# A two-layer decoder trunk: attention of both token tiles of a head at once on all 128 rows, weight roundings pinned in the mixer, tiles moved to multiples of 512 bytes

## The chip, the cores and the metric

The kernel runs on one NeuronCore of a Trainium2 chip. The metric is device time in microseconds (us) of one execution; lower is better. A profile is one execution taken by the hardware profiler: its span goes from the first to the last instruction, and the execution's own time is a little longer than the span. Engines are named as the profile names them: PE is TensorE's matmul, PEld its weight load, DVE is VectorE, ACT is ScalarE, POOL is GpSimd, SP is SyncE, which issues most DMAs.

## What is computed

256 tokens of width 2048 go through two layers. Cut to what matters here, a layer is:

```python
h = rmsnorm(x, attn_norm_g)
q, k, v, gate_b, gate_c, conv_in = split(h @ w_in)          # each 1024 wide
q, k = rmsnorm(q per 64), rmsnorm(k per 64)                 # 8 heads x 2 maps x 64
s = q . k / 8 + bias(relative distance), masked to the past
p = softmax(s)[map 0] - lam * softmax(s)[map 1]             # per head
attn = rmsnorm(p @ v per head) * (1 - lam_init)
conv = gate_b * causal_conv3(gate_c * conv_in)
x = x + concat([attn, conv]) @ w_out
x = x + relu(rmsnorm(x) @ w_up)**2 @ w_down                 # 8192 wide inside
```

All inputs and outputs are float32. The big products are made in float32r, a rounded float32 that PE multiplies in one pass: each operand is split into a rounded part (hi) and what the rounding leaves (lo), and a product is hi*hi + hi*lo + lo*hi.

## The kernel before, in words

**Stages.** For each of the two layers `mixer` (L599) makes everything up to `w_out`, and `mlp` (L667) the rest. In `mixer`, for each half of the heads (four of eight), `linear` (L325) makes q, then k, then v, each 16 row blocks of 128 by 2 token tiles by 3 terms. Then come four column groups of `gate_c` and `conv_in` and four of `gate_b`, by `linear_t` (L344), which turns the product round: the weights are the stationary operand, and the moving one is 512 columns wide (hi and lo of the activations) against hi and 256 against lo. Then `w_out` by `linear`. The multiplication in `mlp` uses `up_part` (L799), which has `linear_t`'s form, `product` (L846) and L969.

**Weights.** `Weights.halves` (L274) takes a loaded block of 128 rows by 1024 numbers and rounds it: an ACT copy to `whi` (L282), then a DVE subtraction to `wlo` (L283). `take` (L310) makes a block's halves three blocks ahead of its use. A block feeds 12 matmuls in `linear`, 8 wide and 8 narrow ones in `linear_t`.

**The order of the work.** PE's order is written out by hand. Small work is a generator that `Background.tick` (L74) carries on a piece at a time: `linear` ticks once in 6 matmuls, `linear_t` four times in a block of 16. `yield n` means: go on n ticks later. The other engines' instructions are ordered by a planner with a cost model of its own; `late(ins)` (L118) pins an instruction behind the one that was written just before it on the same engine.

**Attention.** `qk_norm` (L455) squares, sums and scales q or k, and 8 ticks later transposes each token tile with 4 PE transposes and splits it into hi and lo: one ACT copy and one DVE subtraction on 128 rows by 512 (L481, L482). A head has two maps; map 0 stands on rows 0 to 63 and map 1 on rows 64 to 127. `attention` (L486) then runs `unit(t, i)` for token tile t and head i, eight units for each half, begun 4 ticks apart. A unit makes, for each map, 3 score matmuls on 64 rows (L500) of 128 columns (t = 0) or 256 (t = 1); a DVE pass adds the bias and takes the maximum (L503); ACT takes the exponentials (L510); five small DVE operations follow and the sum of the two maps `p` (L520). 9 ticks later PE transposes `p` (L526: one transpose for t = 0, two for t = 1), ACT and DVE split it, and 4 ticks later 3 or 6 matmuls of 128 columns multiply it with v (L536). The fourth head's unit of each tile evicts the 512 columns of all four heads, norms them, and 9 ticks later transposes them (L562) into `cat`.

**Memory.** Tiles come from pools that lie one behind the other: `const`, `xpool`, `apool` (activations' hi and lo), `wpool` (weights' hi and lo), `nat` (7 buffers of 2 KB a row), `small`, and then the pools of the mixer or of the MLP. Each tile takes a multiple of 32 bytes a row. `const` begins at byte 16,512 of a row, and its tiles take 8,928 bytes, so `xpool` begins at 25,440, which is 352 bytes behind a multiple of 512. All sizes from there on, that of `small` (5,120) too, are multiples of 512. So every operand of the big matmuls begins 352 bytes behind a multiple of 512. `Parts` and the mixer's `bpool` tiles (q, k, v, `cat` and others, 8 buffers of 8 KB) follow the same rule.

Of the kernel before, what the change touches and what calls it, by code (L numbers as in the profile page):

```python
# [9 lines left out]
F32 = mybir.dt.float32  # L10
# [91 lines left out]
def trunk(ctx: ExitStack, tc: tile.TileContext, x, w_in, w_out, conv_w, q_norm_g, k_norm_g,  # L102
# [8 lines left out]
    nat = ctx.enter_context(tc.tile_pool(name="nat", bufs=7))  # L111
# [18 lines left out]

    xs = [xpool.tile([P, NT, CH], F32, tag=f"x{n}", name=f"x{n}") for n in range(D // CH)]
# [9 lines left out]
    ngv = const.tile([NG, P], F32, tag="ngv", name="ngv")  # L141
# [23 lines left out]
    vec = const.tile([ROWS, P], F32, tag="vec", name="vec")  # L165
    nc.gpsimd.dma_start(vec[0:NCW, :], conv_w.rearrange("l i (k p) -> (l i k) p", p=P))
    for i, g in enumerate((q_norm_g, k_norm_g)):
        for m in range(2):
            nc.gpsimd.dma_start(
                vec[QG + i * DEPTH:QG + (i + 1) * DEPTH, m * DK:(m + 1) * DK], g)  # L170
    nc.gpsimd.dma_start(vec[QG + 2 * DEPTH:MG, :], subln_g)
    nc.gpsimd.dma_start(vec[MG:ROWS, :], mlp_norm_g.rearrange("l (k p) -> (l k) p", p=P))
    lamv = const.tile([1, 4, DEPTH, DK], F32, tag="lamv", name="lamv")
    for i, a in enumerate((lambda_q1, lambda_q2, lambda_k1, lambda_k2)):
        nc.gpsimd.dma_start(lamv[:, i], a[None])
    sel = const.tile([NB + 1, REL], F32, tag="sel", name="sel")
    nc.gpsimd.dma_start(sel, selector)
    rel = const.tile([NB + 1, 2 * NH], F32, tag="rel", name="rel")
    nc.vector.memset(rel[NB:NB + 1, :], NEG)
    nc.gpsimd.dma_start(rel[0:NB, :], rel_bias)  # L180
# [15 lines left out]
    def small_setup():  # L196
# [3 lines left out]
        by_dist = const.tile([2 * NH, REL], F32, tag="bydist", name="by_dist")  # L200
# [12 lines left out]
        prod = const.tile([1, 2, DEPTH, DK], F32, tag="lprod", name="lprod")  # L213
# [13 lines left out]
    def load_bias(l, bpool, bias):  # L227

        if l == 0:
            yield from small_setup()  # L230
        revs = []
        for j in range(2):
            rev = bpool.tile([P, NH, S], F32, tag="b", name=f"rev{l}{j}")
            src = by_dist_d[j * NH:(j + 1) * NH, 0:S]
            nc.gpsimd.dma_start(
                rev, bass.AP(src.tensor, src.offset, [[1, P], [REL, NH], [1, S]]))
            revs.append(rev)
        yield 4
        for h in range(0, NH, 2):
            for j in range(2):  # L240
                late(nc.scalar.activation(bias[:, j * NH + h:j * NH + h + 2],
                                          revs[j][:, h:h + 2, ::-1], AF.Copy))
            yield 2
# [21 lines left out]
    class Weights:  # L265
# [8 lines left out]
        def halves(self, raw, c=slice(None)):  # L274
# [11 lines left out]
        cut = False  # L286
# [98 lines left out]
    class Norm:  # L385
# [31 lines left out]
        def factors(self):  # L417
            while not all(t.ready for t in self.tiles):
                yield 1
            tot = small.tile([P, NT], F32, tag="tot", name="tot")  # L420
# [5 lines left out]
            if self.which:  # L426

                self.scale = small.tile([P, 1], F32, tag="rowf2", name="rowf2")
                nc.vector.tensor_mul(self.scale, r[:, 1:2], r[:, 1:2])
                ratio = small.tile([P, 1], F32, tag="ratio", name="ratio")  # L430
# [24 lines left out]
    def qk_norm(acc, r, dst, gain, name):  # L455
# [18 lines left out]
        yield 8  # L474
        for t in range(NT):
            tp = bank(f"{name}tp{t}")
            for i in range(4):
                nc.tensor.transpose(tp[:, i * P:(i + 1) * P], out_[t][:, i * P:(i + 1) * P], ident)
            tp3 = tp.rearrange("p (h c) -> p h c", c=P)
            hi, lo = (dst[:, i, :, t * P:(t + 1) * P] for i in range(2))  # L480
            nc.scalar.activation(hi, tp3, AF.Copy, scale=gain)  # L481
            nc.vector.scalar_tensor_tensor(lo, tp3, gain, hi.bitcast(F32),  # L482
                                           op0=ALU.mult, op1=ALU.subtract)
            yield 1

    def attention(l, qT, kT, v, h0, dst, bias, tmp):  # L486

        parts = dst.open()
        avs, r0s = {}, {}

        def unit(t, i):
            W = (t + 1) * P
            h = h0 + i
            s = tmp.tile([P, 2, S], F32, tag="s", name=f"s{h}_{t}")
            mx = small.tile([P, 2], F32, tag="mx", name=f"mx{h}_{t}")
            su = small.tile([P, 2], F32, tag="su", name=f"su{h}_{t}")
            for m in range(2):
                sc = bank(f"sc{h}_{t}_{m}")
                for n, (a, b) in enumerate(TERMS):
                    nc.tensor.matmul(  # L500
                        sc[:, :W], qT[m * DK:(m + 1) * DK, a, i, t * P:(t + 1) * P],
                        kT[m * DK:(m + 1) * DK, b, i, :W], start=(n == 0), stop=(n == 2))
                nc.vector.tensor_tensor_reduce(  # L503
                    out=s[:, m, :W], in0=sc[:, :W], in1=bias[:, 2 * h + m, S - W:],
                    op0=ALU.add, op1=ALU.max, scale=1.0, scalar=-3.0e38,
                    accum_out=mx[:, m:m + 1])
            nm = small.tile([P, 2], F32, tag="nm", name=f"nm{h}_{t}")
            nc.vector.tensor_scalar_mul(nm, mx, -1.0)
            for m in range(2):
                nc.scalar.activation(s[:, m, :W], s[:, m, :W], AF.Exp, bias=nm[:, m:m + 1],  # L510
                                     accum_out=su[:, m:m + 1])
            rc = small.tile([P, 2], F32, tag="rc", name=f"rc{h}_{t}")
            nc.vector.reciprocal(rc, su)
            if i == 0:
                r0s[t] = small.tile([P, 4], F32, tag="r0", name=f"r0_{h0}_{t}")
            nc.vector.tensor_copy(r0s[t][:, i:i + 1], rc[:, 0:1])
            c = small.tile([P, 1], F32, tag="c", name=f"c{h}_{t}")
            nc.vector.scalar_tensor_tensor(c, su[:, 0:1], rc[:, 1:2], nlam[:, l:l + 1],
                                           op0=ALU.mult, op1=ALU.mult)
            p = tmp.tile([P, S], F32, tag="p", name=f"p{h}_{t}", bufs=2)  # L520
            nc.vector.scalar_tensor_tensor(p[:, :W], s[:, 1, :W], c, s[:, 0, :W],
                                           op0=ALU.mult, op1=ALU.add)
            yield 9
            tp = bank(f"ptp{h}_{t}")
            for b in range(t + 1):
                nc.tensor.transpose(tp[:, b * P:(b + 1) * P], p[:, b * P:(b + 1) * P], ident)  # L526
            pT = tmp.tile([P, 2, S], F32R, tag="pT", name=f"pT{h}_{t}", bufs=2)
            nc.scalar.activation(pT[:, 0, :W], tp[:, :W], AF.Copy)
            nc.vector.tensor_sub(pT[:, 1, :W], tp[:, :W], pT[:, 0, :W].bitcast(F32))
            yield 4  # L530
            if i == 0:
                avs[t] = ps.tile([P, CH], F32, tag="av", name=f"av{h0}_{t}", bufs=1)
            av = avs[t]
            for k in range(t + 1):
                for n, (a, b) in enumerate(TERMS):
                    nc.tensor.matmul(  # L536
                        av[:, i * P:(i + 1) * P], pT[:, a, k * P:(k + 1) * P],
                        v[:, b, k, i * P:(i + 1) * P],
                        start=(k == 0 and n == 0), stop=(k == t and n == 2))
            if i < 3:  # L540
                return
            r0 = r0s[t]
            ao = wide(f"ao{h0}_{t}")
            nc.scalar.activation(ao, av, AF.Copy)
            ss = small.tile([P, 4], F32, tag="ams", name=f"ams{h0}_{t}")
            junk = wide(f"asq{h0}_{t}")
            for b in range(4):
                c = slice(b * P, (b + 1) * P)
                nc.scalar.activation(junk[:, c], ao[:, c], AF.Square, accum_out=ss[:, b:b + 1])
            for _ in range(2):  # L550
                nc.gpsimd.tensor_tensor(ss, ss, r0, op=ALU.mult)
            f = rstd_of(ss, P, f"a{h0}_{t}", 4)
            f2 = small.tile([P, 4], F32, tag="af2", name=f"af2{h0}_{t}")
            nc.gpsimd.tensor_tensor(f2, f, r0, op=ALU.mult)
            an = wide(f"an{h0}_{t}")
            nc.vector.tensor_tensor(
                an.rearrange("p (g d) -> p g d", d=P), ao.rearrange("p (g d) -> p g d", d=P),
                f2.unsqueeze(2).to_broadcast([P, 4, P]), op=ALU.mult)
            yield 9
            tp = bank(f"atp{h0}_{t}")  # L560
            for b in range(4):
                nc.tensor.transpose(tp[:, b * P:(b + 1) * P], an[:, b * P:(b + 1) * P], ident)  # L562
            tp3 = tp.rearrange("p (h c) -> p h c", c=P)
            hi = parts[:, 0, :, t * P:(t + 1) * P]
            nc.scalar.activation(hi, tp3, AF.Copy, scale=s_gain[:, l:l + 1])
            nc.vector.scalar_tensor_tensor(
                parts[:, 1, :, t * P:(t + 1) * P], tp3, s_gain[:, l:l + 1], hi.bitcast(F32),
                op0=ALU.mult, op1=ALU.subtract)
# [458 lines left out]
```

## Time and profile before

| | |
|---|---|
| three runs | 2178.86, 2181.64 and 2182.95 us, median 2181.64 |
| the profiled execution's own time | 2181.14 us |
| its span | 2179.4 us |
| PE matmul busy | 2156.6 us in 11066 matmuls |
| PE weight load busy | 1828.6 us |
| DVE, ACT, POOL busy | 1603.9, 1271.7, 138.8 us |
| mean granted TensorE clock | 0.999 of full |

A busy PE is not PE at its peak, since a matmul's recorded time contains its way through the pipeline: 389 ns are recorded for a 512-column matmul of the down projection, while 576 of them that follow each other take 130.58 us, 226.7 ns each. What a matmul costs the path is therefore read from the distance between starts in the timeline, not from its own duration.

### The profile page before, as it was taken

The page shows a single profiled execution, that of the slowest core. Times are in us where ns is not written, and L with a number is a line of the kernel's source. Part 1 is how long each engine was busy: PE and PEld are TensorE (multiplying, and loading weights), DVE is VectorE, ACT ScalarE, POOL GpSimd, SP SyncE. Part 2 cuts the span into 40 slices and gives each one's busy share as a digit, 9 for nine tenths or more (in the row PEclk, how much of TensorE's full clock was granted, in tenths as well). Part 3 has the DMA queues.
Part 4 walks back from the last instruction along what each step waited for, and adds up shares of the span by engine and source line. Part 5 has one row for each costly group of instructions (what it writes and reads, how often), then busy time and mean ns, then how long its engine had stood idle before and what let it go on. Part 6 is the DMA issues. An engine that isn't in the chain of part 4 may idle for free.

```text
span 2179.4 us, 29050 instructions
## 1 busy us (share of the span) xinstructions
PE 2156.6 (99%) x11066; PEld 1828.6 (84%) x11066; DVE 1603.9 (74%) x2229; ACT 1271.7 (58%) x1718; POOL 138.8 (6%) x194
## 2 busy tenths in 40 slices
PE   8999999999999999999999999999999999999999
PEld 6888888888888888888888888888888888888887
DVE  6677655698888888855566776557988888887554
ACT  6456445566666666654454654455666666665443
POOL 2021100000000000100011111000000000001000
PEclk9999999999999999999999999999999999999999
DMA  7555656476666666587565466656766666666774
GB/s 256 180 156 177 218 185 184 157 238 223 213 212 215 220 208 214 189 277 241 175 205 181 156 199 197 184 173 190 225 218 217 213 212 216 219 208 212 246 242 145
DMA packets 292491, 446.62 MB, mean 205 GB/s; under 512 B 10403, under 2 KB 191221, under 8 KB 292352
## 3 DMA queue, kind: packets, MB, share of 16 engines
q1 hardware_dynamic: 285648, 423.66, 61.5%
q0 software_dynamic: 6656, 21.10, 2.6%
q8 instruction: 86, 1.41, 0.3%
q14 instruction: 53, 0.43, 0.1%
q10 hardware_dynamic: 48, 0.02, 0.0%
HBM read 425.84 MB, written 18.90 MB: 204 GB/s over the span
## 4 chain that ended last, share of the span: by engine, by line
PE 94%; DMA 2%; DVE 2%; ACT 1%; issue 1%; SPq 0%; DVEq 0%; ACTq 0%
PE upc L809 29%; PE dn L969 15%; PE pr L849 13%; PE o L338 8%; PE q L338 4%; PE gc L360 4%; PE ci L360 4%; PE k L338 4%; PE gb L360 4%; PE v L338 4%; PE upw L809 1%; DMA uraw<-in_w_up_dram 1%; PE sc L500 1%; PE av L536 1%; PE tpn L402 1%; DMA draw<-in_w_down_dram 1%
## 5 line engine op out<-in xcount | busy, mean ns | idle before, releaser
L283 DVE TENSOR_TENSOR wlo<-raw,whi 128x1024 fp32r<-128x1024 f32 (+1 forms) x386 | 473.3, 1228 | 385.5 <-ACT whi L282 381.0
L282 ACT ACTIVATE whi<-raw 128x1024 fp32r<-128x1024 f32 (+1 forms) x386 | 406.8, 1055 | 477.8 <-PE dn L969 166.7
L809 PE MATMUL upc<-nT,uhi 128*128 128x512 f32 x1920 | 477.5, 391 | 0.0
L694 ACT ACTIVATE uhi<-uraw 128x1024 fp32r<-128x1024 f32 x256 | 271.2, 1060 | 287.3 <-PE upc L809 253.9
L809 PEld LDWEIGHTS upc<-nT,uhi 128*128 128x128 f32 x1920 | 352.7, 188 | 68.2
L695 DVE TENSOR_TENSOR ulo<-uraw,uhi 128x1024 fp32r<-128x1024 f32 x256 | 312.8, 1222 | 115.3 <-ACT uhi L694 112.9
L969 PE MATMUL dn<-whi,g 128*128 128x512 f32 x1024 | 316.4, 389 | 0.0
L809 PEld LDWEIGHTS upc<-nT,ulo 128*128 128x128 f32 x1920 | 261.9, 190 | 18.7
L809 PE MATMUL upc<-nT,ulo 128*128 128x256 f32 x1920 | 267.7, 282 | 0.0
L969 PEld LDWEIGHTS dn<-whi,g 128*128 128x128 f32 x1024 | 192.2, 188 | 39.7
L969 PE MATMUL dn<-wlo,g 128*128 128x512 f32 x512 | 199.6, 390 | 1.1 <-DVE wlo L283 1.0
L338 PE MATMUL o<-whi,cat 128*128 128x512 f32 x512 | 159.6, 390 | 0.0
L969 PEld LDWEIGHTS dn<-wlo,g 128*128 128x128 f32 x512 | 96.1, 188 | 22.6 <-DVE wlo L283 2.8
L338 PEld LDWEIGHTS o<-whi,cat 128*128 128x128 f32 x512 | 96.2, 188 | 19.7
L338 PE MATMUL o<-wlo,cat 128*128 128x512 f32 x256 | 99.6, 389 | 0.0
L831 POOL DMA_DIRECT2D hid<-h x64 | 34.9, 545 | 949.1 <-ACT h L830 913.4
L849 PE MATMUL pr<-t13h,f 128*128 128x512 f32 x240 | 93.8, 391 | 0.0
L338 PE MATMUL q<-whi,nT 128*128 128x512 f32 x256 | 86.4, 406 | 4.1 <-ACT nT L248 4.1
L338 PE MATMUL k<-whi,nT 128*128 128x512 f32 x256 | 85.3, 399 | 0.0
L849 PE MATMUL pr<-t24h,f 128*128 128x512 f32 x240 | 84.0, 391 | 0.0
L849 PE MATMUL pr<-b2h,f 128*128 128x512 f32 x240 | 84.0, 391 | 0.0
L338 PE MATMUL v<-whi,nT 128*128 128x512 f32 x256 | 83.4, 396 | 0.0
(330 smaller groups left out, 3431.0 us busy)
## 6 DMA issues: line engine op xcount, KB each, us to landing
uraw<-in_w_up_dram SPq DMA_DIRECT2D x128, 1024.0 KB, 5.9
raw<-in_w_in_dram SPq DMA_DIRECT2D x192, 512.0 KB, 3.9
draw<-in_w_down_dram SPq DMA_DIRECT2D x64, 1024.0 KB, 5.1
raw<-in_w_down_dram SPq DMA_DIRECT2D x64, 1024.0 KB, 5.7
raw<-in_w_out_dram SPq DMA_DIRECT2D x64, 512.0 KB, 3.6
hid<-h POOLq DMA_DIRECT2D x64, 256.0 KB, 4.3
back<-hid SPq DMA_DIRECT2D x32, 512.0 KB, 3.3
rev<-by_dist_d POOLq DMA_DIRECT2D x4, 1024.0 KB, 11.1
```

What stands on the lines that cost most here:

```text
L282: nc.scalar.activation(hi[:, k], raw[:, k], AF.Copy)
L283: nc.vector.tensor_sub(lo[:, k], raw[:, k], hi[:, k].bitcast(F32))
L338: nc.tensor.matmul(acc[:, t], a.ap[:, pa, k % KG, t * P:(t + 1) * P], (hi, lo)[pw][:, j], start=(k == 0 and n == 0), stop=(k == nk - 1 and ...
L360: nc.tensor.matmul(acc[:, f, 0] if part else acc[:, f], wt[:, k % 4, fs], a.ap[:, 0, k % KG] if part else a.ap[:, :, k % KG], start=(part ...
L402: nc.tensor.transpose(tp[:, i * S + t * P:i * S + (t + 1) * P], xs[n][:, t, k * P:(k + 1) * P], ident)
L500: nc.tensor.matmul(sc[:, :W], qT[m * DK:(m + 1) * DK, a, i, t * P:(t + 1) * P], kT[m * DK:(m + 1) * DK, b, i, :W], start=(n == 0), stop=(n ...
L694: nc.scalar.activation(hi, src, AF.Copy)
L695: nc.vector.tensor_sub(lo, src, hi.bitcast(F32))
L809: nc.tensor.matmul(acc[:, 0] if part else acc, wt[:, k], a.ap[:, 0, k % KG] if part else a.ap[:, :, k % KG], start=(part == 0 and kh == 0 ...
L831: nc.gpsimd.dma_start(hid[i // 2][:, i % 2 * 2 * S:(i % 2 + 1) * 2 * S], u)
L849: nc.tensor.matmul(prods[n], fs[j][:, pa, a], b[pw], start=(j == 0 and m == 0), stop=(stop and m == 2))
L969: nc.tensor.matmul(acc[:, t], f[:, pa, k, t * P:(t + 1) * P], (hi, lo)[pw][:, k % 2], start=(b == 0 and k == 0 and m == 0), stop=(b == NB2 ...
```

## The change

1. **Scores on 128 rows.** q's tile for a map now holds hi on the map's own 64 rows and lo on the other 64; k's tile `kT` holds hi on both halves of the rows, and a second tile `kL` holds k's lo on the map's own rows and zeros on the others (zeroed by POOL once in each layer). Two matmuls (with `kT`, then `kL`) make what three made before.
2. **A unit is a whole head.** Both token tiles and both maps are made in one unit: 8 score matmuls, 4 bias passes, 4 exponentials, then one negation, reciprocal and copy for both tiles; the first tile's columns stand at 0 to 127 and the second's at 128 to 383 of one score bank and of one `p`. Three transposes, one ACT copy and one DVE subtraction of 384 columns split `p`. Four units for each half start 8 ticks apart; the transposes follow after 10 ticks.
3. **The mixing with v.** `p`'s hi meets v's hi and lo in one matmul of 256 columns, its lo meets v's hi in one of 128: 6 matmuls a head in place of 9. Each head evicts its own columns (ACT copy, DVE addition, two squares). The final norm is made for both tiles together and its transposes follow 12 ticks later, in place of 9.
4. **Splitting q and k.** Each token tile's split takes 2 ACT and 2 DVE operations for q and 4 ACT and 2 DVE for k, all on 64 rows by 512, where one of each on 128 rows did it. It follows 12 ticks behind the norm, in place of 8.
5. **Pinned roundings.** In the mixer every rounding of a weight block (both instructions) goes through `late`.
6. **Memory.** Set-up data (`vec`, `lamv`, `sel`, `rel` and others) move from `const` into one `bpool` buffer of the first layer, `ngv` into `nat`; their loads are written later, inside the first mixer. `nat` has 6 buffers, several tiles of `small` have fewer, and a 224-byte tile `fill` that nothing uses is put into `const`. By the sizes, `const` then takes 1,920 bytes, `xpool` begins at 18,432 = 36 x 512, `small` takes 4,608 = 9 x 512, and every operand of the big matmuls begins at a multiple of 512. The identity of the transposes, inside `const`, does not (352 bytes behind one; before, 128).

```diff
-    nat = ctx.enter_context(tc.tile_pool(name="nat", bufs=7))
+    nat = ctx.enter_context(tc.tile_pool(name="nat", bufs=6))
...
+    const.tile([P, 56], F32, tag="fill", name="fill")
...
             for k in (slice(0, 1), slice(1, None)) if first else (slice(None),):
-                nc.scalar.activation(hi[:, k], raw[:, k], AF.Copy)
-                nc.vector.tensor_sub(lo[:, k], raw[:, k], hi[:, k].bitcast(F32))
+                pair = (nc.scalar.activation(hi[:, k], raw[:, k], AF.Copy),
+                        nc.vector.tensor_sub(lo[:, k], raw[:, k], hi[:, k].bitcast(F32)))
+                if self.keep:
+                    for ins in pair:
+                        late(ins)
...
+    HALF = (slice(0, DK), slice(DK, P))
+    def q_parts(dst):
+        def put(tp3, gain, c):
+            for m, r in enumerate(HALF):
+                hi, lo = dst[r, m, :, c], dst[HALF[1 - m], m, :, c]
+                nc.scalar.activation(hi, tp3[r], AF.Copy, scale=gain[r])
+                nc.vector.scalar_tensor_tensor(lo, tp3[r], gain[r], hi.bitcast(F32),
+                                               op0=ALU.mult, op1=ALU.subtract)
+        return put
+    def k_parts(dst, low):
+        def put(tp3, gain, c):
+            for m, r in enumerate(HALF):
+                hi, lo = dst[r, m, :, c], low[r, m, :, c]
+                nc.scalar.activation(hi, tp3[r], AF.Copy, scale=gain[r])
+                nc.vector.scalar_tensor_tensor(lo, tp3[r], gain[r], hi.bitcast(F32),
+                                               op0=ALU.mult, op1=ALU.subtract)
+                nc.scalar.activation(dst[HALF[1 - m], m, :, c], tp3[r], AF.Copy, scale=gain[r])
+        return put
...
-            for m in range(2):
-                sc = bank(f"sc{h}_{t}_{m}")
-                for n, (a, b) in enumerate(TERMS):
-                    nc.tensor.matmul(
-                        sc[:, :W], qT[m * DK:(m + 1) * DK, a, i, t * P:(t + 1) * P],
-                        kT[m * DK:(m + 1) * DK, b, i, :W], start=(n == 0), stop=(n == 2))
...
+            sc = [bank(f"sc{h}_{m}") for m in range(2)]
+            for flip in range(2):
+                for k in (kT, kL):
+                    for t in range(NT):
+                        W, m = (t + 1) * P, t ^ flip
+                        nc.tensor.matmul(
+                            sc[m][:, OFF[t]:OFF[t] + W], qT[:, m, i, t * P:(t + 1) * P],
+                            k[:, m, i, :W], start=(k is kT), stop=(k is kL))
...
-            yield 9
+            yield 10
...
-            pT = tmp.tile([P, 2, S], F32R, tag="pT", name=f"pT{h}_{t}", bufs=2)
+            pT = tmp.tile([P, 2, 3 * P], F32R, tag="pT", name=f"pT{h}", bufs=1)
...
+            av = ps.tile([P, CH], F32, tag="av", name=f"av{h}", bufs=1)
+            av = av.rearrange("p (t n c) -> p t n c", t=NT, n=2)
+            for t in range(NT):
+                for k in range(t + 1):
+                    w = slice(OFF[t] + k * P, OFF[t] + (k + 1) * P)
+                    nc.tensor.matmul(av[:, t], pT[:, 0, w], v[:, :, k, i * P:(i + 1) * P],
+                                     start=(k == 0), stop=False, skip_group_check=True)
+                    nc.tensor.matmul(av[:, t, 0], pT[:, 1, w], v[:, 0, k, i * P:(i + 1) * P],
+                                     start=False, stop=(k == t), skip_group_check=True)
...
-        yield from staggered([unit(t, i) for t in range(NT) for i in range(4)], 4)
+        yield from staggered([unit(i) for i in range(4)], 8)
...
+            weights.keep = True
...
+            kL = biasp.tile([P, 2, 4, S], F32R, tag="kL", name=f"kL{l}")
+            for m, r in enumerate(HALF):
+                nc.gpsimd.memset(kL[HALF[1 - m], m].bitcast(F32), 0.0)
```

More of the change, by code (lines that the diff above doesn't have):

```diff
@@ L140, in trunk @@
     NG = DEPTH * D // P
-    ngv = const.tile([NG, P], F32, tag="ngv", name="ngv")
+    ngv = wide("ngv")[:NG, :P]
     nc.scalar.dma_start(ngv, attn_norm_g.rearrange("l (k p) -> (l k) p", p=P))
@@ L224, in small_setup, with load_bias @@
         nc.vector.tensor_copy(nlam, lps[:, :DEPTH])
-    def load_bias(l, bpool, bias):
+    def load_bias(l, bpool, bias, setup):
         if l == 0:
-            yield from small_setup()
+            yield from small_setup(*setup)
         revs = []
@@ L419, in factors @@
                 yield 1
-            tot = small.tile([P, NT], F32, tag="tot", name="tot")
+            tot = small.tile([P, NT], F32, tag="tot", name="tot", bufs=1)
             nc.vector.tensor_reduce(tot, self.ss, axis=AX.X, op=ALU.add)
@@ L478, in qk_norm @@
                 nc.tensor.transpose(tp[:, i * P:(i + 1) * P], out_[t][:, i * P:(i + 1) * P], ident)
[L479 to L483, printed above, removed]
+            put(tp.rearrange("p (h c) -> p h c", c=P), gain, slice(t * P, (t + 1) * P))
@@ L484, in qk_norm, with attention @@
             yield 1
-    def attention(l, qT, kT, v, h0, dst, bias, tmp):
+    def attention(l, qT, kT, kL, v, h0, dst, bias, tmp):
         parts = dst.open()
-        avs, r0s = {}, {}
-        def unit(t, i):
-            W = (t + 1) * P
-            h = h0 + i
[L494 to L497, printed above, removed]
-                sc = bank(f"sc{h}_{t}_{m}")
-                for n, (a, b) in enumerate(TERMS):
-                    nc.tensor.matmul(
-                        sc[:, :W], qT[m * DK:(m + 1) * DK, a, i, t * P:(t + 1) * P],
-                        kT[m * DK:(m + 1) * DK, b, i, :W], start=(n == 0), stop=(n == 2))
[L503 to L507, printed above, removed]
-            nc.vector.tensor_scalar_mul(nm, mx, -1.0)
[L509 to L512, printed above, removed]
-            nc.vector.reciprocal(rc, su)
[L514 to L522, printed above, removed]
-            yield 9
-            tp = bank(f"ptp{h}_{t}")
-            for b in range(t + 1):
@@ L530, in unit @@
             yield 4
[L531 to L539, printed above, removed]
+            av = ps.tile([P, CH], F32, tag="av", name=f"av{h}", bufs=1)
@@ new lines, in unit @@
+            av = av.rearrange("p (t n c) -> p t n c", t=NT, n=2)
+            for t in range(NT):
+                for k in range(t + 1):
[4 more added lines that the diff above has]
+                                     start=False, stop=(k == t), skip_group_check=True)
@@ L540, in unit @@
+            low = nat.tile([P, NT, P], F32, tag="wide", name=f"avl{h}")
+            nc.scalar.activation(low, av[:, :, 1], AF.Copy)
+            mine = slice(i * P, (i + 1) * P)
+            nc.vector.tensor_add(ao[:, :, mine], av[:, :, 0], low)
+            for t in range(NT):
+                nc.scalar.activation(low[:, t], ao[:, t, mine], AF.Square,
+                                     accum_out=ss[:, i, t:t + 1])
             if i < 3:
                 return
-            r0 = r0s[t]
-            ao = wide(f"ao{h0}_{t}")
@@ L554, in unit @@
[L554 to L563, printed above, removed]
@@ new lines, in unit @@
+            for _ in range(2):
+                nc.gpsimd.tensor_tensor(flat, flat, rflat, op=ALU.mult)
+            f = rstd_of(flat, P, f"a{h0}", 4 * NT)
+            f2 = small.tile([P, 4, NT], F32, tag="af2", name=f"af2{h0}", bufs=2)
+            nc.gpsimd.tensor_tensor(f2.rearrange("p i t -> p (i t)"), f, rflat, op=ALU.mult)
+            an_ = []
+            for t in range(NT):
+                an = wide(f"an{h0}_{t}")
+                nc.vector.tensor_tensor(
+                    an.rearrange("p (g d) -> p g d", d=P),
+                    ao[:, t].rearrange("p (g d) -> p g d", d=P),
+                    f2[:, :, t:t + 1].to_broadcast([P, 4, P]), op=ALU.mult)
+                an_.append(an)
@@ new lines, in unit @@
+            yield 12
+            for t in range(NT):
+                tp = bank(f"atp{h0}_{t}")
+                for b in range(4):
+                    nc.tensor.transpose(tp[:, b * P:(b + 1) * P], an_[t][:, b * P:(b + 1) * P],
+                                        ident)
+                tp3 = tp.rearrange("p (h c) -> p h c", c=P)
+                hi = parts[:, 0, :, t * P:(t + 1) * P]
+                nc.scalar.activation(hi, tp3, AF.Copy, scale=s_gain[:, l:l + 1])
+                nc.vector.scalar_tensor_tensor(
+                    parts[:, 1, :, t * P:(t + 1) * P], tp3, s_gain[:, l:l + 1], hi.bitcast(F32),
+                    op0=ALU.mult, op1=ALU.subtract)
+                yield 2
@@ L606, in mixer @@
             weights = Weights(rpool)
+            weights.keep = True
             weights.cut = l == 0
+            setup = None
+            if l == 0:
+                setup = setup_loads(bpool.tile([P, 2 * KG * S], F32, tag="b", name="setup"))
             for half in range(2):
@@ L620, in mixer @@
             bias = biasp.tile([P, 2 * NH, S], F32, tag="bias", name="bias")
-            work.start(load_bias(l, bpool, bias), 10)
+            work.start(load_bias(l, bpool, bias, setup), 10)
             hT = norm.tiles
@@ L640, in mixer @@
                                                    op0=ALU.mult, op1=ALU.subtract)
-                work.start(attention(l, qT, kT, v, h0, cat[half], bias, tmp), 3)
+                work.start(attention(l, qT, kT, kL, v, h0, cat[half], bias, tmp), 3)
             cv = bpool.tile([P, AW // P, S], F32, tag="b", name=f"cv{l}")
```

108 lines of the change are left out of this document (67 added, 41 removed).

## The prediction

> **What bounds the kernel now.** I read the page first, its engine rows and the chain that ended last, then PE's own waits.
>
> ```profile
> span 2179.4 us, 29050 instructions
> PE 2156.6 (99%) x11066; PEld 1828.6 (84%) x11066; DVE 1603.9 (74%) x2229; ACT 1271.7 (58%) x1718; POOL 138.8 (6%) x194
> PE 94%; DMA 2%; DVE 2%; ACT 1%; issue 1%; SPq 0%; DVEq 0%; ACTq 0%
> ```
> ```profile
> PE q L338 <- ACT nT L248: 4.1, 1, 4.1
> PE gps L152 <- POOL ident masks.py:199: 3.5, 1, 3.5
> PE up L809 <- ACT ev L819: 3.2, 2, 2.0
> ```
>
> The reader is to see that PE is the path: 94% of the last chain is its matmuls, and all its waits together are 18 us, none of them in attention or for a weight block of the mixer. So the change is worth what it takes off PE's own sequence, unless it makes PE wait. A matmul's price is the distance between starts, from the chain of the down projection (576 of 512 columns in 130.58 us: 226.7 ns each) and the timeline of the gate stage:
>
> ```profile
> 957.33 130.58 PE dn L969 x576
> ```
> ```profile
> 208.22 1.11 PE L360 MATMUL gc<-nT,wlo 128*128 128x256 f32 x8
> 209.17 2.00 PE L360 MATMUL ci<-nT,whi 128*128 128x512 f32 x8
> ```
>
> Eight of 256 columns take 209.17 - 208.22 = 0.95 us, 119 ns each. The timeline around one head's second tile gives attention's prices:
>
> ```profile
> 134.68 0.39 PE L338 MATMUL k<-wlo,nT 128*128 128x512 f32 x1
> 134.91 0.39 PE L338 MATMUL k<-whi,nT 128*128 128x512 f32 x1
> 135.22 0.62 PE L500 MATMUL sc<-kT,qT 64*128 64x256 f32 x6
> 135.78 0.50 PE L338 MATMUL k<-whi,nT 128*128 128x512 f32 x1
> ...
> 137.06 0.39 PE L338 MATMUL k<-whi,nT 128*128 128x512 f32 x1
> 137.29 0.78 PE L536 MATMUL av<-v,pT 128*128 128x128 f32 x6
> 137.91 0.41 PE L526 MATMUL ptp<-ident,p 128*128 128x128 f32 x2
> 138.07 0.48 PE L338 MATMUL v<-whi,nT 128*128 128x512 f32 x1
> ...
> 139.31 0.62 PE L338 MATMUL v<-whi,nT 128*128 128x512 f32 x2
> ```
>
> From 134.68 to 137.29 PE did 8 projection matmuls and the six scores: 2.61 - 8 x 0.2267 = 0.80 us for the scores, although six of 256 columns alone would be 0.71. From 137.06 to 139.31, 6 projection matmuls, the mixing and two transposes: 2.25 - 1.36 = 0.89. Likewise six scores of 128 columns (106.98 to 109.50) cost 0.71, three mixing matmuls with one transpose (109.27 to 111.78) 0.47, and six mixing matmuls alone (157.45 to 159.50) 0.69, that is 115 ns for one of 128 columns. The small scores cost nearly as much as the wide: most of it is going in and out. After the scores the next projection matmuls start 0.34, 0.24 and 0.24 us apart in place of 0.227.
>
> **The change, part by part.**
>
> *Scores and mixing, on the path.* A head costs 0.71 + 0.80 + 0.47 + 0.89 = 2.87 us. New: scores 4 x 0.115 + 4 x 0.119 = 0.94; mixing 3 x 0.115 + 3 x 0.119 = 0.70; three transposes in one go, priced as the one and the two were (0.47 - 0.345 = 0.125, and 0.20), 0.33. Sum 1.97, so 0.90 us a head and 16 heads: **14.4 us less**. No row shows a 128-row score matmul. Nearest rows: the mixing's (115, also float32r on 128 rows), which I take, as going between equal 128-row forms shows no dearer step in that row; if each group instead keeps the scores' going in and out (0.71 against 6 x 0.057, the closest two mixing starts at 109.50, leaves 0.37 us), one such step a head is 16 x 0.37 = 6 us back. At best four 128-column matmuls hide in the wide ones' spacing: 16 x 7 x 0.058 = 6.5 us more.
>
> On this step the Trainium skill speaks against the change. Its page "TensorEngine Tiling (Array Packing)", section "When to Use Tiling", says that a contraction of 64 rows or fewer should be split by rows, since the two halves of the array then run side by side, up to twice as fast. By it the twelve scores of a head are six slots, some 3 x 0.115 + 3 x 0.119 = 0.70 us, the eight new ones cost 0.94, and the scores lose 0.24 x 16 = 4 us in place of gaining 9. The trace has 0.71 + 0.80 = 1.51 for them, so the row decides.
>
> *Splits of q and k.* For each token tile ACT has 4 more and DVE 2 more, at 0.68 us (L481) and 0.75 (L482): for 4 halves of 2 tiles 21.8 us on ACT and 12 on DVE, both layers. Cover: in the windows 40 to 85 us ACT is busy 25.6 of 45 us and DVE 28.3. k's split begins 12 ticks behind k, is 8 x 0.68 = 5.4 us of ACT with some three roundings (1.06 each) between, 8.6 us in all; the scores follow at tick 19, 7 x 1.36 = 9.5 us later. It just fits; I take 0 to 1 us of wait at each of four places. All uncovered: 22 us.
>
> *A whole head in a unit.* Between scores and transposes lie, by the shapes' means, bias 2 x (0.286 + 0.083) + 2 x (0.419 + 0.083) = 1.74, negation 0.17, exponentials 2 x 0.58 + 2 x 0.69 = 2.54, reciprocal and copy 0.31, two factors and sums 0.55 + 0.35 + 0.48 = 1.38: 6.1 us, where the second tile alone had 3.6. Ten ticks are 13.6 us in the projections. In the gate stage, where the second half's units run, four ticks are 8 x 0.227 + 8 x 0.119 = 2.77 us, so ten are 6.9, and some 2 us of attention's own matmuls lie between. Some 2.8 us are left for roundings, which are one of 1.06 (ACT) and one of 1.23 (DVE) in 2.77 us, and part of these fall into the other engine's turn. I take 0 here as well, with rival 2 for its loss.
>
> *Pinned roundings.* No row has PE wait for a mixer's block, so nothing is to be gained. Behind a pinned rounding wait the next rounding and, through them, PE three blocks later (8 us); behind a held ACT exponential the roundings wait in turn. The loads on SP's queue wait for the roundings (SP's longest wait, L298 on wlo, 422 us in all) and keep three blocks' lead. At nothing.
>
> *Memory.* The set-up loads come later on POOL's queue, before anything on it that PE needs (rps at 26.9 us); kL's zeroing is POOL's, busy 6%. Evictions by head in place of by half: off the path. Fewer `nat` buffers: no wait in the trace names them. At nothing. The address: before, every operand of the big matmuls stands 352 bytes behind a multiple of 512, so no row shows another. Bound: a cost by the read, not by the column, can be at most 2 x 119 - 227 = 11 ns a matmul. The matmuls of 512 columns are 7628 (2048 of L809, 1920 of L338, 1536 of L969, 1260, 768, 96): 86 us at most, with the 2816 of 256 columns 118. The other end is 0; a loss is excluded since moving and stationary operands shift alike. I take 0: the spacing of 226.7 is the same at every stage, with weights now moving and now stationary.
>
> The Trainium skill is divided. "SBUF — State Buffer", section "Specifications (TRN2)", gives lines of 16 bytes; 352 is a multiple of 16, so by it the shift is worth nothing. "TensorE: Matmul & The Clock Gate", section "Wait — 56ns, not 53.3ns?", gives 215.7 ns for 512 columns; were the address the whole difference, 7628 x 11 ns = 84 us would go and the sum be some 2084.
>
> *Sum.* The profiled execution took 2181.1 us (span 2179.4), close to the median 2181.6. 2181.1 - 14.4 + 1 for k's splits = **2168 us**.
>
> **Rivals.**
>
> 1. *The address is a cost of every read.* For: twice the spacing of 256 columns is 238, not 227, so something is paid by the matmul and not by the column, and all operands share one odd remainder. Against: nothing varies with it. 2168 - 86 = 2082 (2050 with the narrow ones).
> 2. *Slower: the longer chain in the gate stage.* PE waits at each of the four transposes of the second half, in both layers. For: 6.1 us of chain in 6.9 us of ticks, with DVE already busy 12.05 of 14 us from 166 to 180. Against: before, PE never waits there. With three roundings on each engine wholly in the way, 6.9 - 2.8 = 4 us; at 3 us a unit 8 x 3 = 24, so 2191. It decides from 14.4 / 8 = 1.8 us a unit.
> 3. *The gain is eaten:* the same wait at 1.3 to 2.3 us a unit: 2178 to 2186.
> 4. *The scores keep their steps,* or the waits for k are a few us: 2174. This lies in the forecast's own range, 2159 to 2177.
>
> **How the numbers follow.** Forecast 0.48, rival 1 0.27, rival 2 0.14, rival 3 0.11. Within 0.2% (4.4 us, what a measurement of this kernel tells from none) holds rival 3 and little else: 0.12; slower 0.15; faster 0.73. The range goes from 2065, which leaves out the far part of rival 1, to 2190, which leaves out half of rival 2.
>
> **What would show it.** Right: one score group of 8 at about 0.94 us and a head at 2.0 in the timeline; the down projection still 226.7 ns apart; PE's waits still near 18 us. Rival 1: 512-column spacing at 216 in every stage. Rivals 2 and 3: ptp on a DVE sum, or sc on a split of k, in PE's waits. I am wrong if the total moves while neither spacing nor these waits do.

## The result and the profile after

| | before | after |
|---|---|---|
| median | 2181.73 us (6 runs, 2178.86 to 2182.95) | 2210.30 us (6 runs, 2204.41 to 2215.03) |
| the profiled execution's own time, its span | 2181.14, 2179.4 us | 2209.14, 2207.4 us |
| mean granted TensorE clock | 0.999 | 0.994 |

The ratio is 1.0131, interval [1.0120, 1.0141]: slower by 1.3%. The prediction was 2168 us with a range from 2065 to 2190, so it missed the side and the range. First the page of the changed kernel: its span, its engines and the shares of the chain that ended last.

```profile
span 2207.4 us, 28808 instructions
PE 2158.2 (98%) x10954; PEld 1831.6 (83%) x10954; DVE 1608.8 (73%) x2197; ACT 1291.0 (58%) x1742; POOL 143.1 (6%) x178
PE 89%; DVE 5%; ACT 3%; issue 1%; DMA 1%; POOL 1%; DVEq 0%; SPq 0%; ACTq 0%
```

PE has 112 matmuls fewer and is busy 1.6 us longer, and DVE's and ACT's shares of the chain have grown (before, 2% and 1%). The waits of PE in the changed kernel (us in total, times, longest) say where:

```profile
PE v L353 <- DVE wlo L295: 13.4, 4, 3.4
PE k L353 <- DVE wlo L295: 11.9, 6, 3.4
...
PE q L353 <- DVE wlo L295: 2.4, 1, 2.4
...
PE sc L542 <- ACT kT L493: 1.5, 2, 0.8
```

13.4 + 11.9 + 2.4 = 27.7 us are waits of the mixer's q, k and v for the low half of a weight block; before had none in the mixer. Attention has only the 1.5 us at `sc`, no wait at `ptp`. The spacing of the big matmuls has not moved, by the chain of the changed kernel (start us, us, what, times):

```profile
967.33 130.58 PE dn L1032 x576
```

130.58 us for 576, to the hundredth what it was.

**How a rounding comes late.** The timeline of DVE in the changed kernel, first layer, where k's norm falls into v's projection (start us, us, instruction, then in brackets the idle time before it and who ended it):

```profile
65.97 1.22 DVE L295 TENSOR_TENSOR wlo<-raw,whi 128x1024 fp32r<-128x1024 f32 x1 [0.61 <-ACT whi L294]
67.12 0.68 DVE L504 TENSOR_REDUCE k00ms<-k00sq 128x8 f32<-128x512 f32 x1
69.84 0.23 DVE L508 TENSOR_SCALAR k00f<-k_r,rowf 128x8 f32<-128x8 f32 x1 [2.04 <-POOL k_r L397]
70.17 0.69 DVE L510 TENSOR_TENSOR k00n<-k,k00f 128x512 f32<-128x512 f32 x1
71.62 0.69 DVE L504 TENSOR_REDUCE k00ms<-k00sq 128x8 f32<-128x512 f32 x1 [0.76 <-ACT k00sq L502]
74.35 0.23 DVE L508 TENSOR_SCALAR k00f<-k_r,rowf 128x8 f32<-128x8 f32 x1 [2.04 <-POOL k_r L397]
74.61 0.69 DVE L510 TENSOR_TENSOR k00n<-k,k00f 128x512 f32<-128x512 f32 x1
75.22 1.22 DVE L295 TENSOR_TENSOR wlo<-raw,whi 128x1024 fp32r<-128x1024 f32 x1
```

The same place in the kernel before:

```profile
63.34 1.23 DVE L283 TENSOR_TENSOR wlo<-raw,whi 128x1024 fp32r<-128x1024 f32 x1 [1.50 <-ACT whi L282]
64.48 0.68 DVE L463 TENSOR_REDUCE k00ms<-k00sq 128x8 f32<-128x512 f32 x1
66.06 1.23 DVE L283 TENSOR_TENSOR wlo<-raw,whi 128x1024 fp32r<-128x1024 f32 x1 [0.90 <-ACT whi L282]
67.20 0.23 DVE L467 TENSOR_SCALAR k00f<-k_r,rowf 128x8 f32<-128x8 f32 x1
67.47 0.69 DVE L469 TENSOR_TENSOR k00n<-k,k00f 128x512 f32<-128x512 f32 x1
68.78 1.23 DVE L283 TENSOR_TENSOR wlo<-raw,whi 128x1024 fp32r<-128x1024 f32 x1 [0.62 <-ACT whi L282]
```

Each token tile's norm sends a sum to POOL for a power and takes it back (L504, then L508), and DVE sits idle for 2.04 us meanwhile. Before, the planner put a rounding into that gap: the one at 66.06 stands between the sum and the scaling, and the scaling then waits for nothing. Pinned, a rounding keeps its written place, and the norm of both tiles is written in one piece. So the rounding stands behind two such gaps and a third of 0.76 us: from 65.97 to 75.22 are 9.25 us from one rounding to the next. `wpool` has room for three blocks, and the block that PE is using is one of them. PE in the changed kernel, same place:

```profile
64.63 0.39 PE L353 MATMUL v<-whi,nT 128*128 128x512 f32 x1
...
72.34 0.39 PE L353 MATMUL v<-wlo,nT 128*128 128x512 f32 x1
72.57 0.61 PE L353 MATMUL v<-whi,nT 128*128 128x512 f32 x2
76.49 0.80 PE L353 MATMUL v<-wlo,nT 128*128 128x512 f32 x1 [3.31 <-DVE wlo L295]
77.09 1.05 PE L353 MATMUL v<-whi,nT 128*128 128x512 f32 x2
```

PE begins v's first block at 64.63, and the rounding at 65.97 makes the third. Three blocks last 3 x 2.72 = 8.2 us, so at 72.8 they are used up, 6.8 us after that rounding began. The next low half is ready at 75.22 + 1.22 = 76.44, 3.6 us too late; 3.31 us of it are recorded as PE's wait. ACT's half of that block is late too, though not as late: the pinned `whi` starts at 71.49, behind a square for which ACT had idled 4.24 us.

The matmul behind the wait records 0.80 us in place of 0.39. The busy time of the engines by stretches tells why (after the length come PE, PEld, DVE, ACT and POOL busy, the granted clock, the DMA share and GB/s):

```profile
76.00:79.40 3.40, 2.91 (x7) 2.33 (x8) 2.71 (x3) 0.00 (x0) 0.00 (x0) 0.50 0.51 151
79.40:84.00 4.60, 4.60 (x22) 3.77 (x21) 1.22 (x1) 1.66 (x2) 0.00 (x0) 1.00 0.68 231
```

After a wait of 3.31 us PE gets half its clock for 3.40 us. There are five such stretches of 3.4 us and one of 6.8, 23.8 us in all; at half speed at most half of it is lost, **11.9 us**.

**The account.** A head now costs 0.947 (eight scores) + 0.72 (mixing) + 0.365 (three transposes) = 2.03 us by the distances of the neighbouring starts, against 2.84 to 2.87 before: 16 heads give 13 us back. 27.7 + 11.9 + 1.5 - 13 = 28.1; the spans differ by 28.0. That they meet so closely is partly chance, since 11.9 is an upper bound and the sum leaves out that PE's other waits are 2.7 us shorter than before. By recorded time alone PE's waits grew from 17.7 to 44.2 us and its busy time by 1.6 us, again 28.1.

### The profile page after: what moved, and what is told of

Its sections match the earlier page's. It is cut to its first block, busy times and chain, and to the rows that moved or that the text cites. A ratio compares the mean times of both kernels' runs of the same rounds, so it can differ in the third digit from the quotient of the medians.

```text
span 2207.4 us, 28808 instructions
## 1 busy us (share of the span) xinstructions
PE 2158.2 (98%) x10954; PEld 1831.6 (83%) x10954; DVE 1608.8 (73%) x2197; ACT 1291.0 (58%) x1742; POOL 143.1 (6%) x178
## 4 chain that ended last, share of the span: by engine, by line
PE 89%; DVE 5%; ACT 3%; issue 1%; DMA 1%; POOL 1%; DVEq 0%; SPq 0%; ACTq 0%
PE upc L872 29%; PE dn L1032 15%; PE pr L912 13%; PE o L353 8%; PE q L353 4%; PE ci L375 4%; PE gb L375 4%; PE gc L375 4%; PE k L353 2%; PE v L353 2%; DVE wlo L295 1%; PE upw L872 1%; PE sc L542 1%; DMA back<-hid 1%; POOL k_r L397 1%
## 5 line engine op out<-in xcount | busy, mean ns | idle before, releaser
L353 PE MATMUL v<-whi,nT 128*128 128x512 f32 x256 | 88.4, 417 | 0.0
```

The source lines that it names most:

```text
L353: nc.tensor.matmul(acc[:, t], a.ap[:, pa, k % KG, t * P:(t + 1) * P], (hi, lo)[pw][:, j], start=(k == 0 and n == 0), stop=(k == nk - 1 and ...
```

## The experiments

The theory after the result: the pins alone make the loss, and the attention is worth what was forecast. Its rivals: that the new attention's own DVE and ACT work holds the roundings up, and that the move to other addresses costs or gives something that the loss hides.

**1. The change without the pins.**

```diff
-            weights.keep = True
+            weights.keep = False
```

> The changed kernel with the roundings of weights left to the planner, all else as changed. Pin theory (the pinned low rounding waits on DVE behind the whole norm of q or k, so PE runs out of weight blocks in the k and v stages): the eight waits of PE on the low rounding go, the six k and v stages that became 2 to 6 us longer fall back, and the attention's saving stays: 2167 us, between 2160 and 2176. Rival, longer chain or more split work: the stages stay long without pins, 2200 to 2212. Rival, the pins protect from a bad order of the planner: 2215 or more.

2172.46 us, ratio 0.9966 [0.9954, 0.9978]. PE's waits in this kernel:

```profile
PE sc L542 <- ACT kT L493: 3.9, 2, 2.0
...
PE av L584 <- DVE ao L591: 3.3, 2, 1.7
```

No wait of q, k or v for `wlo`, a granted clock of 1.0, and PE is busy 2144.6 us where the changed kernel's is 2158.2 with the same 10954 matmuls: 13.6 us less of recorded time, a little over the 11.9 that the half clock costs at most (the first matmul behind a wait is also recorded longer, 0.50 us at 50.16 in the changed kernel, at full clock). Against the kernel before, PE is busy 12.0 us less, near the 13 us read for the 16 heads. By the two medians the pins cost 2210.3 - 2172.5 = 38 us. What is left of PE's waits in attention (3.9 + 3.3 us) was foreseen in part; runs 8 to 10 take it up.

**2. The kernel before with the pins alone.** The rounding pair of before goes through `late` as in the change; nothing else.

> The kernel before with the same pins in the mixer and nothing else. Pin theory: the waits in the k and v stages appear here too, about the 37 us that the changed kernel's long stages add up to, 2210 to 2222. Rival, new attention: the pins cost nothing on the old attention, 2179 to 2184.

2220.0 us, ratio 1.0187 [1.0171, 1.0202]. PE's waits:

```profile
PE k L341 <- DVE wlo L283: 12.8, 4, 3.4
PE v L341 <- DVE wlo L283: 10.4, 4, 3.3
```

The same waits at the same places (with 2.4 at q, 25.6 us), without the new attention: the rival that blames the attention's own work falls, but for some 2 us of waits. 2220.0 - 2180.2 = 40 us for the pins here, 38 there.

**3 and 4. The address alone, both ways.** The kernel before with its operands moved to multiples of 512, by a filler and `ngv` moved to `nat`; and the changed kernel with the operands back at 352 behind a multiple.

```diff
# run 3, in the kernel before
+    const.tile([P, 40], F32, tag="fill", name="fill")
-    ngv = const.tile([NG, P], F32, tag="ngv", name="ngv")
+    ngv = wide("ngv")[:NG, :P]
# run 4, in the changed kernel
-    const.tile([P, 56], F32, tag="fill", name="fill")
+    const.tile([P, 16], F32, tag="fill", name="fill")
```

> The kernel before with every operand of the big matmuls at a multiple of 512 bytes (a 160-byte filler in const, ngv moved into nat), and nothing else. The forecast: 2181 within 0.2%, 512-column spacing 226.7 ns. Rival 1 of the prediction: 2082 to 2100, spacing about 216 ns.

> The changed kernel with a filler of 64 in place of 224 bytes, so that the big operands stand 352 bytes behind a multiple of 512 as they did before. If the address is worth nothing: 2204 to 2215, as changed. If it is worth something: longer by it, up to 86 us.

Run 3: 2178.81 us, 0.9994 [0.9985, 1.0002]. Run 4: 2208.57 us, 1.0137 [1.0121, 1.0153], which overlaps the changed kernel's own interval. The down projection in the chain of run 3:

```profile
954.60 130.58 PE dn L971 x576
```

Nothing moved, in either direction.

**5 and 6. One pin of the pair.** Only the low half (DVE) pinned, then only the high half (ACT).

```diff
-                    for ins in pair:
-                        late(ins)
+                    late(pair[1])          # run 5; run 6: late(pair[0])
```

> The changed kernel with only the low roundings (DVE) pinned. If the DVE pin carries the loss (the low rounding behind both tiles' norm on DVE): 2200 to 2212, with most of the eight waits of PE. If it is the ACT pin: 2168 to 2178.

> The changed kernel with only the high roundings (ACT) pinned. If the DVE pin carries the loss: 2168 to 2180, as ACT's part of the norm holds the high rounding by some 5 us, within the 8 us that three blocks last. If ACT's pin does: 2200 or more.

Both missed the ranges expected for a loss that DVE's pin carries. Run 5: 2222.63 us, 1.0197 [1.0183, 1.0211], dearer than both pins. Run 6: 2190.82 us, 1.0049 [1.0034, 1.0065], 18 us above the kernel without pins. So ACT's pin is not free, though the expectation had put it so. PE's waits of run 6:

```profile
PE v L352 <- DVE wlo L295: 4.3, 6, 0.8
...
PE k L352 <- ACT whi L294: 3.9, 2, 2.0
PE v L352 <- ACT whi L294: 3.4, 2, 1.7
PE k L352 <- DVE wlo L295: 2.9, 4, 0.8
```

14.5 us of waits, now partly for the high half, and by the granted clock up to 7 us lost at half rate. What holds the high half stands in ACT's timeline, just before PE's wait of 1.7 us in v:

```profile
153.83 0.31 ACT L592 ACTIVATE avl<-ao 128x128 f32<-128x128 f32 x1 [3.46 <-DVE ao L590]
...
154.43 2.94 ACT L294 ACTIVATE whi<-raw 128x1024 fp32r<-128x1024 f32 x3
```

Three pinned roundings stand behind the squares of attention's output, for which ACT idled 3.46 us until DVE had made `ao`; the 2.0 us wait in k has the same row before it, with 2.59 us. In run 5 the place of the surplus can be read: against the changed kernel, v and k wait 2.1 us more for `wlo`, `sc` waits 6.4 us for `kT` in place of 1.5, and the stretches at half clock add up to 37.5 us in place of 23.8, which is up to 6.8 us more. Together these are up to 13.8 us, and the spans differ by 12.8. ACT's timeline in the first layer shows what makes `kT` later: left free, ACT runs three roundings and a copy of v among the eight copies of k's split (173.61 to 184.48), where the changed kernel has one rounding and that copy (171.40 to 179.85); two roundings are 2.1 of the 2.4 us by which the wait is longer.

**7. The pins kept, the chain ahead of them shortened.** `qk_norm` is written for both tiles side by side: squares and sums, then both powers, then both scalings. The work is the same.

```diff
             nc.vector.tensor_reduce(ms, sq.rearrange("p (g d) -> p g d", d=DK),
                                     axis=AX.X, op=ALU.add)
-            f = rstd_of(ms, DK, f"{name}{t}", NH)
+            mss.append(ms)
+        for t in range(NT):
+            fs_.append(rstd_of(mss[t], DK, f"{name}{t}", NH))
+        for t in range(NT):
+            rt = r[:, t:t + 1]
...
-            nc.vector.tensor_scalar_mul(f2, f, rt)
+            nc.vector.tensor_scalar_mul(f2, fs_[t], rt)
```

> The changed kernel with its pins, but the norm of q and k written for both token tiles at once: both squares and sums, then both powers on POOL, then both scalings. DVE's stretch between two low roundings shrinks from 9.2 to about 5.7 us. If it is the length of that stretch that starves PE: the 3.3 us waits and the half-clock stretches behind them go, 2167 to 2182. If pins cost in another way (every pinned pair serializes ACT and DVE): above 2195.

2179.51 us, 0.9998 [0.9989, 1.0007]: 31 of the 38 us are back with every pin in place. The timeline of DVE in this kernel, same place:

```profile
64.66 1.27 DVE L504 TENSOR_REDUCE k00ms<-k00sq 128x8 f32<-128x512 f32 x2
67.38 0.23 DVE L512 TENSOR_SCALAR k00f<-k_r,rowf 128x8 f32<-128x8 f32 x1 [1.45 <-POOL k_r L397]
...
69.42 0.23 DVE L512 TENSOR_SCALAR k00f<-k_r,rowf 128x8 f32<-128x8 f32 x1 [1.09 <-POOL k_r L397]
...
70.29 3.49 DVE L295 TENSOR_TENSOR wlo<-raw,whi 128x1024 fp32r<-128x1024 f32 x3
```

The stretch without a rounding shrinks from 67.12 to 75.22, 8.1 us, to 64.66 to 70.29, 5.6 us, and three roundings then run in a row. PE's wait at this place falls from 3.31 to 0.84 us, those of q, k and v for `wlo` from 27.7 to 9.7 us, and one stretch at half clock is left of the six. The new order also takes away the 4.24 us for which ACT idled before its second square, so the run does not divide the gain between the two engines. In this kernel a pin's price thus follows the length of what is written ahead of it.

**8, 9 and 10. No pins, and room for attention's chains.** Without pins, the splits of q and k come 9 ticks behind the norm in place of 12 (run 9), attention starts at tick 5 in place of 3 (run 10), or both (run 8).

```diff
-            weights.keep = True
+            weights.keep = False
-        yield 12                    # in qk_norm; runs 8 and 9
+        yield 9
-                work.start(attention(l, qT, kT, kL, v, h0, cat[half], bias, tmp), 3)
+                work.start(attention(l, qT, kT, kL, v, h0, cat[half], bias, tmp), 5)   # runs 8 and 10
```

> The changed kernel without pins, with the transposes of q and k 9 ticks behind the norm in place of 12, and attention begun 5 ticks behind v in place of 3: room for the split of k. What PE still waited without pins was 3.9 us for k's split and 3.3 us for the bank of the mixing. If the first goes: 2166 to 2170 where the run without pins had 2172; the second should stay. If the later start only moves the waits: 2171 to 2176.

> The first of the two edits of the run with room, alone: no pins, transposes of q and k after 9 ticks, attention begun 3 ticks behind v as in the change. k's split then begins 3 ticks (4 us) earlier, so the 2.0 us waits of the first scores for it should go and the later start should not be needed: 2165 to 2169. If the planner's order is what changed: 2171 to 2174, as the run without pins alone.

> The second edit alone: no pins, transposes of q and k after 12 ticks, attention begun 5 ticks behind v. Two ticks are 2.7 us in the projections and 1.4 to 1.8 us in the gate stage, where the wait was 2.0: most of the first scores' waits go, 2167 to 2171; the bank's waits stay.

| | us | ratio to before |
|---|---|---|
| neither (run 1) | 2172.46 | 0.9966 [0.9954, 0.9978] |
| 9 ticks (run 9) | 2168.23 | 0.9946 [0.9932, 0.9960] |
| start at 5 (run 10) | 2169.74 | 0.9950 [0.9936, 0.9964] |
| both (run 8) | **2164.83** | 0.9931 [0.9919, 0.9944] |

Run 8 beats both kernels, and its expected range. PE's longest waits in it:

```profile
PE gps L155 <- POOL ident masks.py:199: 3.5, 1, 3.5
PE q L353 <- ACT nT L260: 2.5, 1, 2.5
PE pr L912 <- DVE f L904: 1.8, 2, 1.0
```

The waits of `sc` and of `av` on `ao` are gone, though the second was expected to stay in runs 8 and 10; but for 0.7 us at `av` on `pT`, what is left belongs to the beginning, the MLP and the norms. Each step alone leaves something: run 9 still has 3.3 us at `av` and 1.4 at `sc` for `qT`, run 10 has two waits of 1.1 us at the transposes of q. The scores of one head in the timeline of PE in run 8:

```profile
1173.79 0.39 PE L542 MATMUL sc<-kT,qT 128*128 128x128 f32 x2
1174.02 0.40 PE L542 MATMUL sc<-kL,qT 128*128 128x128 f32 x2
1174.25 0.39 PE L542 MATMUL sc<-kT,qT 128*128 128x128 f32 x2
1174.48 0.39 PE L542 MATMUL sc<-kL,qT 128*128 128x128 f32 x2
1174.71 0.39 PE L353 MATMUL q<-whi,nT 128*128 128x512 f32 x1
```

1174.71 - 1173.79 = 0.92 us for all eight, a narrow and a wide one in each row of 0.23 us, with no step on going in or out.

## Why the prediction was wrong, step by step

**The step that failed** is the one on pinned roundings. It put them "At nothing", since "No row has PE wait for a mixer's block, so nothing is to be gained". It even named the path of a loss ("Behind a pinned rounding wait the next rounding and, through them, PE three blocks later (8 us)"), but it asked for the length of nothing that would now stand ahead of a rounding: it named a held ACT exponential, and not the norm on DVE. The absence of waits before was no cover of its own: it was the planner's work, which filled the 2.04 us gaps of the norm with roundings. The rows for it were in the trace of before: the rounding at 66.06 stands inside a norm. Two POOL gaps, one ACT gap and the norm's own DVE work are 9.25 us from rounding to rounding, and the rounding itself takes 1.22 more, against 6.8 us of work that PE had left. The forecast's 8 us were too many as well, since one of the three blocks is already in use when the third is rounded. Runs 1 and 2 show 38 and 40 us from the pins alone, run 7 that a shorter chain ahead of them gives 31 us back.

**The size of the loss** had a second part that no row of before could give: the half clock behind the waits, up to 11.9 us.

- *Scores, mixing, transposes*: 0.947, 0.72 and 0.365 us against the forecast's 0.94, 0.70 and 0.33; 13 us saved against 14.4. Right, and in PE's recorded time, 12.0 us less in run 1 than before, too. The row of the mixing matmuls carried over to 128-row scores, and the bound with a dear step on going in and out falls by the lines of run 8.
- The Trainium skill's "TensorEngine Tiling (Array Packing)", section "When to Use Tiling", would split a contraction of 64 rows by rows. Here that does not pay, and not because the halves fail to run side by side. In the kernel before, the six scores of the second tile start in three pairs, 0.01 us apart within a pair (of the group at 135.22, two have started by 135.25 and four by 135.46). The last two pairs begin 0.12 us apart, and three such steps would be 0.35 us, but the group takes 0.80. The rest lies at its ends: 0.32 us from the last projection matmul to the first score and 0.34 between the first two projection matmuls behind, in place of 0.227, and 0.22 between the first two pairs. (The forecast's 0.37 us for going in and out took the six as one behind the other.) So eight full-row matmuls at 0.92 to 0.95 us are cheaper than twelve half-row ones at 1.51, and the forecast was right to go by the row.
- *k's and q's splits*: "0 to 1 us of wait at each of four places"; the changed kernel has 1.5 us at two of the places in all, run 1 two waits of 2.0 us. Right in kind, a little small without the pins; run 8 shows that three ticks and two ticks of room take it away.
- *The whole-head chain in the gate stage, and rivals 2 and 3*: the stage of `gc` and `ci` fell from 101.7 to 100.0 us and no `ptp` wait is among PE's, so their place was wrong. Without pins, PE waits twice for 1.7 us at `av` for the head before it (run 1), which no step had.
- *Memory and the address*: worth 0, as put. Rival 1, which held 0.27 of the chances, falls by runs 3 and 4, and so does its 2082 us.
- *What stayed the same*: 226.7 ns for 512 columns, by the chain of the down projection, in eleven of the twelve kernels and 227.1 in run 5.
- *"I am wrong if the total moves while neither spacing nor these waits do"* is what came: the waits were at a place that the list did not have.

Without its pins the change is the forecast's kernel, at 2172.5 us against 2168. That it comes so near is in part luck: PE waits 7.2 us at `sc` and `av` where 1 was put and the heads save 1.4 us less, but PE's other waits are 3.5 us shorter than before, which no step had. With room for the chains it is at 2164.8.

**What stays open.** Why the planner, with ACT free, puts two more roundings into k's split in run 5; and how the loss of the changed kernel divides between DVE's chain and ACT's, since one pin alone costs 18 us (run 6) and the other 50 (run 5), and both 38. Runs 9 and 10 gain 4.2 and 2.7 us over run 1 and run 8 gains 7.6: the steps add, within the spread.

## What to carry to other kernels

A pin on prefetch work costs nothing only as long as everything written ahead of it on its engine, idle gaps included, is shorter than what PE still has in hand when that work begins; so before pricing an order that is taken from a planner, look for what the planner has put into the gaps of a chain between engines. Where such an order must be kept, shorten the chain ahead of it (both tiles' links side by side gave 31 of 38 us back). Price short groups of matmuls by the distances in their surroundings: full-row matmuls without a change of shape were cheaper than the half-row ones they replace, though there are only a third fewer of them and the half-row ones ran two at a time.

## What the runs showed of the hardware that was not expected

**A short wait of PE can cost more than itself, depending on where it falls.** Five more stretches at half clock show it in the changed kernel, by the same columns as above; three of them:

```profile
161.30:164.70 3.40, 3.40 (x9) 2.63 (x8) 2.36 (x2) 2.44 (x3) 0.00 (x0) 0.50 0.51 164
1110.20:1113.60 3.40, 3.40 (x10) 2.62 (x9) 2.17 (x6) 0.00 (x0) 0.92 (x2) 0.50 0.97 283
...
1257.00:1263.80 6.80, 5.78 (x14) 4.52 (x15) 3.66 (x4) 3.27 (x7) 0.00 (x0) 0.50 0.44 140
```

PE is busy through the first two and does 9 or 10 matmuls in 3.40 us, where 15 of 512 columns fit at 226.7 ns. The stretches are 3.4 us or twice that, whatever the wait. By the trace's record of the granted clock the six begin on one grid: from the start at 75.96 the others are 25, 303, 314, 322 and 346 steps of 3.4133 us away. Not every wait is followed by one. Three steps of that grid at full clock, the first two around PE's wait of 3.30 us that ends at 50.16, the third in the wait of 3.31 us that ends at 76.49:

```profile
45.24:48.65 3.41, 1.62 (x8) 0.99 (x6) 1.28 (x3) 3.41 (x7) 1.83 (x2) 1.00 0.01 2
48.65:52.06 3.41, 1.90 (x8) 1.60 (x9) 3.41 (x4) 2.57 (x5) 0.00 (x0) 1.00 0.23 54
72.55:75.96 3.41, 0.63 (x3) 0.19 (x1) 1.58 (x3) 1.87 (x2) 1.68 (x2) 1.00 0.00 0
```

The first wait is split, 1.8 and 1.5 us idle, and the clock stays full; the second lies almost whole in one step, 2.8 us idle, and half clock follows. In the twelve traces, their first and last 15 us left out, every step at full clock in which PE idled 2.0 us or more was followed by one at half clock, and none below 1.6 us; between them both occur. Run 1's two waits of 2.0 us at `sc` left at most 1.6 us idle in one step, and its clock stayed at full.

The Trainium skill's "TensorE: Matmul & The Clock Gate", section "What's actually happening", says that the clock is gated to half by how busy PE was, over a free-running window of about 3.4 us. The lengths of 3.40 and 6.80 us, the clock of 0.50 and the grid agree with it: a window that runs free makes some waits costly and others not.

**A power on POOL is long for its size.** POOL takes 1.64 us for a power of 128 x 8 numbers (L397), and DVE idles 2.04 us for the result, three times its own pass over 128 x 512 (0.69 us).
